# Attention scores: the lower part of the keys on 128 partitions instead of 64

## The chip, the cores and the metric

The kernel runs on one core of a Trainium2 chip. The metric is the device time of one execution in microseconds; the number compared is the median of several runs. A core has the matrix engine (PE, with its weight loads shown apart as PEld), the vector engine (DVE), the scalar engine (ACT), GpSimd (POOL) and the queues that issue DMAs (SP, and those of ACT and POOL).

## The reference

The reference is one inference step of a decoder trunk of two layers. Layer 0 mixes tokens by a gated delta rule, layer 1 by attention in a sliding window; each is followed by a gated MLP, and a norm stands at the end. 512 prompt tokens and 8 samples of 4 tokens go through the same weights, all in float32. What matters here is the prompt's attention: 16 query heads of 64, 4 key heads, blocks of 128 queries that see their own and the previous 128 keys.

```python
s = jnp.einsum('bnqkgd,bnskd->bnkgqs', qb, kk)            # queries x (previous block, own block)
mask = band[None] & ((blkid > 0) | (j[None] >= W))        # band: 0 <= rel <= 128
s = s * SWA_SCALE - alibi_slopes() * rel
m = jnp.maximum(jnp.max(s, -1, keepdims=True), sinks)
p = jnp.exp(s - m); p = p / (p.sum(-1) + exp(sinks - m))
o = jnp.einsum('bnkgqs,bnskd->bnqkgd', p, vv)
```

## The kernel before

Tokens lie along the free axis (544 of them: 512 and 32), features on the 128 partitions. A dense product (`dense`, L140, its matmul at L159) splits each float32 operand into an upper part in the format float32r and the rest, the lower part, and sums three matmuls: upper by upper, upper by lower, lower by upper. Weights come in pieces of 512 columns by DMA (`load_w`, L126) and are split by ACT (L133) and DVE (L135). Tokens are worked in two halves of 256 and 288 columns.

The attention (`attention`, L1125) goes through a plan written out by hand (L39): `kv` projects keys and values, `q0` to `q7` project two query heads each, `a0` to `a7` do the scores, softmax and value product of those two heads, `s0` and `s1` do the samples, `w0` and `w1` the output projection. The framework then orders the instructions of every engine at build time, by its own estimate of when each can start, so that the matmuls of projections come between those of scores. On the chip each engine keeps that order.

In `proj_kv` (L1184) the keys of two heads lie on one tile, 64 partitions each, for a = 0 and 1. `upper` (L1176) makes the upper part on ACT, in one buffer. L1190 subtracts it on DVE and so makes the lower part `kl`, 128 partitions by 2 x 512 columns. L1193 copies the upper part by DMA (four for each a, on the queues of SP and ACT) so that each head c of `kh` holds the same 64 rows twice, on both halves of the partitions. `proj_q` (L1206) lays the queries out to match: for head c the upper part of the queries lies on half c and their lower part on the other half (L1214 to L1216).

In `prompt` (L1221) each block of 128 queries and 128 or 256 keys is then the sum of two matmuls into one place:

```python
PE.matmul(sl, lhsT=q[:, c, ...], rhs=kh[:, c, a, ks], start=True, stop=False)      # L1241
PE.matmul(sl, lhsT=q[rows, c, ...], rhs=kl[rows, a, ks], start=False, stop=True)   # L1242
```

L1241 has 128 rows and gives both products with the keys' upper part; L1242 has the 64 rows of head c, on which the queries' upper part and the keys' lower part lie. There are 64 such pairs, 8 in each of the 8 prompt steps. A score bank (`sc`, two of them) holds two blocks. DVE adds the bias and takes the maximum (L1243); ACT does the exp (L1254); DVE scales (L1264); PE transposes (L1266) into banks that ACT copies out (L1267); PE multiplies with the values (L1272). POOL clears the sample queries' tile (L1152), computes the norm's reciprocal root as a power (L214) and copies sample queries (L1219).

Of the kernel before, what the change touches and what calls it, by code (L numbers as in the profile page):

```python
# [9 lines left out]
F32 = mybir.dt.float32  # L10
F32R = mybir.dt.float32r
BF16 = mybir.dt.bfloat16
AF = mybir.ActivationFunctionType
ALU = mybir.AluOpType

P = 128
SEQ = 512
# [58 lines left out]
def kernel(  # L76
# [315 lines left out]

    ffn(0, 1)
    attention(tc, locals())
    ffn(1, 3)

# [728 lines left out]
def attention(tc, env):  # L1125
    nc, PE, DVE, ACT, POOL = (env[k] for k in ("nc", "PE", "DVE", "ACT", "POOL"))
# [6 lines left out]
    with ExitStack() as ctx:  # L1133
        env["psum_pools"](ctx, acc=ACC, sc=2, pt=PT, po=1, sp=1)
        c1 = ctx.enter_context(tc.tile_pool(name="a1", bufs=1))
# [7 lines left out]
        kT = c1.tile([P, 2, TOK], F32, name="kT")  # L1143

        kh = c1.tile([P, 2, 2, SEQ], F32R, name="kh")
        kl = c1.tile([P, 2, SEQ], F32R, name="kl")
        bqs = c1.tile([P, 8], F32, name="bqs")
        DVE.tensor_scalar(bqs, pc("bqkv", 0, 8), 0.125, None, ALU.mult)
        vt = c1.tile([P, 5, 256], F32, name="vt")
# [5 lines left out]
        def operand(qi):  # L1155

            if qi not in ops:
                if qi < 4:
                    ops[qi] = [c1.tile([P, TOK], F32R, name=f"ao{r}{qi}") for r in "hl"]
                else:  # L1160
                    ops[qi] = [hpool.tile([P, TOK], F32R, tag=f"h{r}{qi}", name=f"ao{r}{qi}") for r in "hl"]
            return ops[qi]

        def proj(m, out, scale=None, tag="acc"):
            ps = dense(w_qkv[m], f"wqkv{m}", hrhs, [8], tag=tag)
            t = tmp("pre", f"qkv{m}")[:, :TOK]
            for p, o, r in halves(ps, t, rstd):
                DVE.tensor_tensor(o, p, r, ALU.mult)
            if scale is None:
                DVE.tensor_scalar(out, t, pc("bqkv", m), None, ALU.add)  # L1170
            else:
                ACT.activation(out, t, AF.Identity, bias=bqs[:, m:m + 1], scale=scale)
# [3 lines left out]
        def upper(t, name):  # L1176
            hi = p2.tile([P, SEQ], F32R, tag="hi", name=f"hi{name}", bufs=1)
            ACT.copy(hi, t)
            return hi

        def spread(out, t, d):
            (nc.sync if d else nc.scalar).dma_start(out.bitcast(F32), t.bitcast(F32))

        def proj_kv():  # L1184
            for a in range(2):
                proj(8 + a, kT[:, a], tag=("acc", "sc")[a])
            nc.gpsimd.dma_start(kT_out, kT[:, :, SEQ - P:TOK])
            for a in range(2):
                hi = upper(kT[:, a, :SEQ], f"k{a}")
                DVE.tensor_tensor(kl[:, a], kT[:, a, :SEQ], hi, ALU.subtract)  # L1190
                for c in range(2):
                    for d in range(2):
                        spread(kh[64 * d:64 * d + 64, c, a], hi[64 * c:64 * c + 64], d)  # L1193
            for a in range(2):
                vT = tmp("y", f"vT{a}")[:, :TOK]
                proj(10 + a, vT)
                nc.gpsimd.dma_start(vT_out[:, a], vT[:, SEQ - P:TOK])
                pv = bank("pt", f"pvt{a}")
                for n in range(NCH):
                    PE.transpose(pv[:, n * P:(n + 1) * P], vT[:, n * P:(n + 1) * P], ident)  # L1200
                ACT.copy(vt[:, 0:4, a * P:(a + 1) * P], pv.rearrange("p (n c) -> p n c", n=NCH))
                pv2 = bank("pt", f"pvs{a}")
                PE.transpose(pv2[:32, 0:P], vT[:, SEQ:TOK], ident)
                ACT.copy(vt[:32, 4, a * P:(a + 1) * P], pv2[:32, 0:P])
# [16 lines left out]
        def prompt(qi):  # L1221

            a, g = qi // 4, qi % 4
            q = q_[qi]
            bias = p2.tile([P, 2, 256], F32, tag="bias", name=f"bias{qi}")
            for c in range(2):
                DVE.tensor_scalar(bias[:, c], ka[:, 0:256], SLOPES[(2 * a + c) * 4 + g], None, ALU.mult)
            s = p2.tile([P, 2, NCH, 256], F32, tag="s", name=f"s{qi}")
            mx = p2.tile([P, 2, NCH], F32, tag="mx", name=f"mx{qi}")
            es = p2.tile([P, 2, NCH], F32, tag="es", name=f"es{qi}")  # L1230
            sm = p2.tile([P, 2, NCH], F32, tag="sm", name=f"sm{qi}")
            for n0 in range(0, NCH, 2):
                for c in range(2):
                    rows = slice(64 * c, 64 * c + 64)
                    h = (2 * a + c) * 4 + g
                    pss = bank("sc", f"ps{qi}_{n0}_{c}")
                    for n in (n0, n0 + 1):
                        k0 = P if n == 0 else 0
                        sl = pss[:, (n - n0) * 256 + k0:(n - n0 + 1) * 256]
                        ks = slice((n - 1) * P + k0, (n + 1) * P)  # L1240
                        PE.matmul(sl, lhsT=q[:, c, n * P:(n + 1) * P], rhs=kh[:, c, a, ks], start=True, stop=False)  # L1241
                        PE.matmul(sl, lhsT=q[rows, c, n * P:(n + 1) * P], rhs=kl[rows, a, ks], start=False, stop=True)  # L1242
                        DVE.tensor_tensor_reduce(  # L1243
                            s[:, c, n, k0:], sl, bias[:, c, k0:], 1.0, pc("sink", h),
                            ALU.add, ALU.max, mx[:, c, n:n + 1])
            for c in range(2):
                h = (2 * a + c) * 4 + g
                DVE.tensor_scalar(es[:, c], mx[:, c], -1.0, pc("sink", h), ALU.mult, ALU.add)
            DVE.tensor_scalar(mx, mx, -1.0, None, ALU.mult)
            ACT.activation(es, es, AF.Exp)  # L1250
            for n in range(NCH):
                for c in range(2):
                    k0 = P if n == 0 else 0
                    ACT.activation(s[:, c, n, k0:], s[:, c, n, k0:], AF.Exp, bias=mx[:, c, n:n + 1],  # L1254
                                   accum_out=sm[:, c, n:n + 1])
            DVE.tensor_tensor(sm, sm, es, ALU.add)
            DVE.reciprocal(sm, sm)
            po = bank("po", f"po1{qi}")
            for n in range(NCH):
                ptp = bank("pt", f"ptp{qi}_{n}")  # L1260
                pT = p2.tile([P, 2, 256], F32, tag="pT", name=f"pT{qi}_{n}")
                k0 = P if n == 0 else 0
                for c in range(2):
                    DVE.tensor_scalar(s[:, c, n, k0:], s[:, c, n, k0:], sm[:, c, n:n + 1], None, ALU.mult)  # L1264
                    for kb in range(k0 // P, 2):
                        PE.transpose(ptp[:, c * 256 + kb * P:c * 256 + (kb + 1) * P], s[:, c, n, kb * P:(kb + 1) * P], ident)  # L1266
                ACT.copy(pT[:, :, k0:], ptp.rearrange("p (c k) -> p c k", c=2)[:, :, k0:])  # L1267
                for c in range(2):
                    rows = slice(64 * c, 64 * c + 64)
                    kv = 2 * a + c  # L1270
                    for kb in range(k0 // P, 2):
                        PE.matmul(po[rows, n * P:(n + 1) * P], lhsT=vt[:, n - 1 + kb, kv * 64:kv * 64 + 64],  # L1272
                                  rhs=pT[:, c, kb * P:(kb + 1) * P], start=(kb == k0 // P), stop=(kb == 1))
            oh, ol = operand(qi)
            ACT.copy(oh[:, :SEQ], po)
            DVE.tensor_tensor(ol[:, :SEQ], po, oh[:, :SEQ], ALU.subtract)
# [65 lines left out]
        def w_out(part):  # L1342
# [13 lines left out]
            if part == 1:  # L1356
                for m in range(4, KD):
                    norm_split(3, m, x[m])

        steps = {"q": proj_q, "a": prompt, "s": sample, "w": w_out}  # L1360
        for step in PLAN_A.split():
            if step == "kv":
                proj_kv()
            else:
                steps[step[0]](int(step[1:]))
# [171 lines left out]
```

## Time and profile before

| | |
|---|---|
| median of 3 runs | 1753.47 us (1748.12 to 1753.71) |
| the profiled execution's own time | 1754.97 us |
| its span | 1753.2 us |
| PE busy | 1648.0 us, 94% of the span |
| PEld busy | 1577.9 us, 90% |
| DVE busy | 947.7 us, 54% |
| ACT busy | 754.0 us, 43% |
| POOL busy | 230.0 us, 13% |
| mean granted clock of PE | 0.961 |

The span runs from the first to the last instruction. Busy times are sums over instructions and overlap between engines. Matmuls overlap each other, and their ends are modelled; the distance between the starts of two matmuls tells the pace of PE better than their durations. The form of a matmul is written as rows*columns of its weights and then rows x columns of what moves through: `64*128 64x256` has 64 rows, 128 columns of weights and 256 moving columns. [...]

### The profile page before, as it was taken

The page shows a single profiled execution, that of the slowest core. Times are in us where ns is not written, and L with a number is a line of the kernel's source. Part 1 is how long each engine was busy: PE and PEld are TensorE (multiplying, and loading weights), DVE is VectorE, ACT ScalarE, POOL GpSimd, SP SyncE. Part 2 cuts the span into 40 slices and gives each one's busy share as a digit, 9 for nine tenths or more (in the row PEclk, how much of TensorE's full clock was granted, in tenths as well). Part 3 has the DMA queues.
Part 4 walks back from the last instruction along what each step waited for, and adds up shares of the span by engine and source line. Part 5 has one row for each costly group of instructions (what it writes and reads, how often), then busy time and mean ns, then how long its engine had stood idle before and what let it go on. Part 6 is the DMA issues. An engine that isn't in the chain of part 4 may idle for free.

```text
span 1753.2 us, 33971 instructions
## 1 busy us (share of the span) xinstructions
PE 1648.0 (94%) x13370; PEld 1577.9 (90%) x13370; DVE 947.7 (54%) x2071; ACT 754.0 (43%) x1822; POOL 230.0 (13%) x474
## 2 busy tenths in 40 slices
PE   7997996898897899999999999999999999999997
PEld 6996896897786798999999999998779999999997
DVE  7985485467465646654444433456566554454333
ACT  5864484474555445433333323245444332332221
POOL 2216118106402500100000000000000000000001
PEclk9998898999898899999999999999799999999999
DMA  6232431442443464622322333443112233223332
GB/s 233 85 82 65 126 100 51 112 138 62 102 155 109 112 195 140 214 89 86 91 90 85 91 87 92 125 138 86 43 43 73 85 91 89 87 87 90 90 88 85
DMA packets 138487, 179.31 MB, mean 102 GB/s; under 512 B 58600, under 2 KB 66840, under 8 KB 136280
## 3 DMA queue, kind: packets, MB, share of 16 engines
q1 hardware_dynamic: 131096, 155.95, 30.7%
q0 software_dynamic: 3104, 14.67, 2.3%
q10 hardware_dynamic: 4128, 6.53, 1.2%
q8 instruction: 105, 1.72, 0.4%
q14 instruction: 54, 0.44, 0.1%
HBM read 146.84 MB, written 25.02 MB: 98 GB/s over the span
## 4 chain that ended last, share of the span: by engine, by line
PE 77%; POOL 7%; DMA 7%; ACT 4%; DVE 3%; issue 2%; SPq 1%; POOLq 0%; ACTq 0%; DVEq 0%
PE wg_p L159 15%; PE wu_p L159 15%; PE wd_p L159 14%; PE win_p L159 5%; PE wo_p L159 5%; PE wqkv_p L159 4%; DMA Lb<-D 3%; PE wz_p L159 3%; POOL Tn L733 3%; PE wao_p L159 3%; POOL subt L731 3%; PE ps L1242 1%; PE po L1272 1%; PE ptp L1266 1%; PE wdl_p L372 1%
## 5 line engine op out<-in xcount | busy, mean ns | idle before, releaser
L159 PE MATMUL wu_p<-hl,wh_wu 128*128 128x256 f32 (+1 forms) x704 | 199.7, 288 | 0.0
L159 PE MATMUL wg_p<-hl,wh_wg 128*128 128x256 f32 (+1 forms) x704 | 199.7, 288 | 0.0
L159 PE MATMUL wg_p<-hh,wl_wg 128*128 128x256 f32 (+1 forms) x704 | 199.2, 287 | 0.0
L159 PE MATMUL wu_p<-hh,wl_wu 128*128 128x256 f32 (+1 forms) x704 | 199.1, 287 | 0.0
L159 PE MATMUL wg_p<-hh,wh_wg 128*128 128x256 f32 (+1 forms) x704 | 198.5, 288 | 0.3 <-DVE g L329 0.3
L159 PE MATMUL wu_p<-hh,wh_wu 128*128 128x256 f32 (+1 forms) x704 | 198.8, 288 | 0.0
L159 PE MATMUL wd_p<-al,wh_wd 128*128 128x256 f32 (+1 forms) x660 | 190.4, 289 | 0.0
L159 PE MATMUL wd_p<-ah,wl_wd 128*128 128x256 f32 (+1 forms) x660 | 190.1, 288 | 0.0
L159 PE MATMUL wd_p<-ah,wh_wd 128*128 128x256 f32 (+1 forms) x660 | 188.1, 285 | 0.0
L135 DVE TENSOR_TENSOR wl_wd<-wr_wd,wh_wd 128x512 fp32r<-128x512 f32 x90 | 58.3, 648 | 151.7 <-ACT wh_wd L133 150.6
L159 PE MATMUL win_p<-hh0n,wh_win 128*128 128x256 f32 (+1 forms) x448 | 134.3, 302 | 2.0 <-ACT pre L541 2.0
L159 PE MATMUL win_p<-hl0n,wh_win 128*128 128x256 f32 (+1 forms) x448 | 135.0, 303 | 0.7 <-DVE hl0n L278 0.7
L159 PEld LDWEIGHTS wg_p<-hh,wh_wg 128*128 128x128 f32 x704 | 132.3, 188 | 0.4 <-DVE g L329 0.4
L159 PEld LDWEIGHTS wg_p<-hh,wl_wg 128*128 128x128 f32 x704 | 132.6, 189 | 0.0
L159 PEld LDWEIGHTS wu_p<-hh,wl_wu 128*128 128x128 f32 x704 | 132.6, 189 | 0.0
L159 PE MATMUL win_p<-hh0n,wl_win 128*128 128x256 f32 (+1 forms) x448 | 132.4, 299 | 0.0
L159 PEld LDWEIGHTS wu_p<-hh,wh_wu 128*128 128x128 f32 x704 | 132.4, 188 | 0.0
L159 PEld LDWEIGHTS wg_p<-hl,wh_wg 128*128 128x128 f32 x704 | 132.4, 188 | 0.0
L159 PEld LDWEIGHTS wu_p<-hl,wh_wu 128*128 128x128 f32 x704 | 132.4, 188 | 0.0
L133 ACT CAST wh_wg<-wr_wg 128x512 fp32r<-128x512 f32 x88 | 54.7, 621 | 178.6 <-PE wu_p L159 130.8
L133 ACT CAST wh_wd<-wr_wd 128x512 fp32r<-128x512 f32 x90 | 52.8, 586 | 174.7 <-PE wd_p L159 153.8
L159 PEld LDWEIGHTS wd_p<-al,wh_wd 128*128 128x128 f32 x660 | 124.1, 188 | 0.0
(452 smaller groups left out, 4506.3 us busy)
## 6 DMA issues: line engine op xcount, KB each, us to landing
wr_wg<-in_w_gu SPq DMA_DIRECT2D x88, 256.0 KB
wr_wu<-in_w_gu SPq DMA_DIRECT2D x88, 256.0 KB
wr_wd<-in_w_dn SPq DMA_DIRECT2D x75, 256.0 KB
wr_win<-in_w_in SPq DMA_DIRECT2D x64, 256.0 KB
Sg<-in_sdelta SPq DMA_DIRECT2D x8, 1024.0 KB
wr_wz<-in_w_in SPq DMA_DIRECT2D x32, 256.0 KB
out_ss<-Sg POOLq DMA_DIRECT2D x8, 1024.0 KB, 5.4
wr_wo<-in_w_out SPq DMA_DIRECT2D x32, 256.0 KB
```

The lines of the kernel that those rows point to most:

```text
L133: ACT.copy(hi[:, :n], raw[:, o:o + n])
L135: DVE.tensor_tensor(lo[:, :n], raw[:, o:o + n], hi[:, :n], ALU.subtract)
L159: PE.matmul(ps[f][:m, :hw(f)], lhsT=wt[:, sl], rhs=xt[:, hc(f)], start=(k0 + j == 0 and wi == 0), stop=(k0 + j == total - 1 and wi == 2),)
L372: PE.matmul(p, lhsT=wt[i][:, sl], rhs=xt[k][:, c], start=(k == 0 and wi == 0), stop=(k == KF - 1 and wi == 2))
L731: POOL.tensor_tensor(tv, Lb[:, j, j + 1:32].unsqueeze(2).to_broadcast([P, r_, w]), Tn[:, j, 0:w].unsqueeze(1).to_broadcast([P, r_, w]), AL ...
L733: POOL.tensor_tensor(Tn[:, j + 1:32, 0:w], Tn[:, j + 1:32, 0:w], tv, ALU.subtract)
L1242: PE.matmul(sl, lhsT=q[rows, c, n * P:(n + 1) * P], rhs=kl[rows, a, ks], start=False, stop=True)
L1266: PE.transpose(ptp[:, c * 256 + kb * P:c * 256 + (kb + 1) * P], s[:, c, n, kb * P:(kb + 1) * P], ident)
L1272: PE.matmul(po[rows, n * P:(n + 1) * P], lhsT=vt[:, n - 1 + kb, kv * 64:kv * 64 + 64], rhs=pT[:, c, kb * P:(kb + 1) * P], start=(kb == k0 ...
```

## The change

The tile of the keys' lower part gets one copy for each of the two heads c, with the other head's 64 partitions zero. POOL writes the zeros once, ahead of the attention's other work. The subtraction on DVE writes head by head, on 64 partitions each. The second score product then reads all 128 rows of the queries, as the first does; the rows that it adds are multiplied by zero. The number of matmuls and their columns stay as they are.

```diff
-        kl = c1.tile([P, 2, SEQ], F32R, name="kl")
+        kl = c1.tile([P, 2, 2, SEQ], F32R, name="kl")
+        for c in range(2):
+            POOL.memset(kl[64 * c:64 * c + 64, 1 - c].bitcast(F32).rearrange("p a s -> p (a s)"), 0.0)
...
             for a in range(2):
                 hi = upper(kT[:, a, :SEQ], f"k{a}")
-                DVE.tensor_tensor(kl[:, a], kT[:, a, :SEQ], hi, ALU.subtract)
                 for c in range(2):
+                    rows = slice(64 * c, 64 * c + 64)
+                    DVE.tensor_tensor(kl[rows, c, a], kT[rows, a, :SEQ], hi[rows], ALU.subtract)
                     for d in range(2):
                         spread(kh[64 * d:64 * d + 64, c, a], hi[64 * c:64 * c + 64], d)
...
                         PE.matmul(sl, lhsT=q[:, c, n * P:(n + 1) * P], rhs=kh[:, c, a, ks], start=True, stop=False)
-                        PE.matmul(sl, lhsT=q[rows, c, n * P:(n + 1) * P], rhs=kl[rows, a, ks], start=False, stop=True)
+                        PE.matmul(sl, lhsT=q[:, c, n * P:(n + 1) * P], rhs=kl[:, c, a, ks], start=False, stop=True)
```

## Rows read from the trace of the kernel before

**Rows 1.** The page: its head, and the chain that ended last by engine.
```profile
span 1753.2 us, 33971 instructions
...
PE 77%; POOL 7%; DMA 7%; ACT 4%; DVE 3%; issue 2%; SPq 1%; POOLq 0%; ACTq 0%; DVEq 0%
```

**Rows 2.** Stretches: length, PE, PEld, DVE, ACT, POOL busy, clock, DMA share, GB/s.
```profile
1160.00:1237.00 77.00, 77.00 (x569) 65.13 (x567) 45.93 (x171) 39.99 (x109) 4.01 (x14) 1.00 0.39 110
1237.00:1268.00 31.00, 30.98 (x158) 21.82 (x159) 17.90 (x89) 13.74 (x49) 0.00 (x0) 0.67 0.01 1
1268.00:1303.00 35.00, 34.81 (x265) 29.05 (x264) 21.40 (x73) 16.76 (x50) 0.00 (x0) 1.00 0.14 46
```

**Rows 3.** PE's longest wait from 1160 to 1320 us: total, times, longest one.
```profile
PE ptp L1266 <- DVE s L1264: 0.9, 1, 0.9
```

**Rows 4.** Timeline of PE (start, duration): a pair of 256 columns among dense matmuls.
```profile
1164.39 0.28 PE L1241 MATMUL ps<-kh,qp 128*128 128x256 f32 x1
1164.60 0.38 PE L1242 MATMUL ps<-kl,qp 64*128 64x256 f32 x1
1164.91 0.40 PE L159 MATMUL wqkv_p<-hh,wl_wqkv 128*128 128x288 f32 x1
1165.14 0.29 PE L159 MATMUL wqkv_p<-hh,wh_wqkv 128*128 128x288 f32 x1
1165.28 0.29 PE L159 MATMUL wqkv_p<-hl,wh_wqkv 128*128 128x288 f32 x1
```

**Rows 5.** Timeline of the weight loads in the same place.
```profile
1164.60 0.18 PEld L1242 LDWEIGHTS ps<-kl,qp 64*128 64x128 f32 x1 [0.15 <-issue]
1165.02 0.19 PEld L159 LDWEIGHTS wqkv_p<-hh,wh_wqkv 128*128 128x128 f32 x1
```

**Rows 6.** The tile `kl`: its readers on PE (ns min/median/max, first and last start).
```profile
L1242 PE MATMUL ps<-kl,qp x64: 322/381/580, 1160.9 to 1302.7; 64*128 64x256 f32 x48, 64*128 64x128 f32 x16
```

**Rows 7.** Timeline of PE: one pair behind another.
```profile
1283.34 0.39 PE L1241 MATMUL ps<-kh,qp 128*128 128x256 f32 x1
1283.66 0.38 PE L1242 MATMUL ps<-kl,qp 64*128 64x256 f32 x1
```

**Rows 8.** Timeline of PE at the lower clock: a pair, and two dense matmuls.
```profile
1240.61 0.58 PE L1242 MATMUL ps<-kl,qp 64*128 64x256 f32 x1
1241.12 0.58 PE L1241 MATMUL ps<-kh,qp 128*128 128x256 f32 x1
...
1264.15 0.41 PE L159 MATMUL wao_p<-aol,wh_wao 128*128 128x256 f32 x1
1264.37 0.41 PE L159 MATMUL wao_p<-aoh,wl_wao 128*128 128x256 f32 x1
```

**Rows 9.** Timeline of PE: a pair of 128 columns.
```profile
1160.72 0.22 PE L1241 MATMUL ps<-kh,qp 128*128 128x128 f32 x1
1160.87 0.32 PE L1242 MATMUL ps<-kl,qp 64*128 64x128 f32 x1
```

**Rows 10.** Groups by form, 1060 to 1340 us: busy us, mean ns, idle before.
```profile
L1254 ACT ACTIVATE s<-s,mx 128x256 f32<-128x256 f32 x48 | 23.7, 497 | 0.0
...
L1243 DVE CUSTOM_DVE_ANT_0 s<-ps,bias,par 128x256 f32<-128x256 f32 x48 | 23.0, 482 | 25.8 <-PE ps L1242 25.3
```

**Rows 11.** The tile `kl`: its writer; then the chain around it (start, duration, what).
```profile
L1190 DVE TENSOR_TENSOR kl<-kT,hik x2: 684/688/693, 1135.0 to 1141.5; 128x512 fp32r<-128x512 f32 x2
...
1135.12 5.59 DMA kh<-hik
...
1141.58 0.57 issue
1142.15 0.46 DVE qkv L1168
```

**Rows 12.** Timeline of POOL (start, duration, idle before and what ended it).
```profile
1119.24 0.53 POOL L1152 MEMSET qd<- 128x512 f32 x1 [384.77 <-PE wd_p L159]
1126.27 1.20 POOL L214 TENSOR_TENSOR ny<-nv,mhalf 128x5 f32<-128x5 f32 x1 [6.50 <-DVE nv L228]
```

## The prediction

> **What bounds the kernel now.** I read first the page's head and its chain of waits, then a table of the attention by stretches, then PE's waits there, then single matmuls. The profiled execution took 1754.97 us, its span 1753.2 [rows 1], so 1.8 us lie around the span; the median of the three runs is 1753.47, 1.5 us below this execution. PE holds 77% of the chain that ended last [rows 1]. The score products (L1241, L1242) all start between 1160 and 1303 us. [...] From 1160 to 1320 the longest wait of PE is 0.9 us, for DVE's scaled probabilities behind the last scores [rows 3]. So PE's own instruction stream sets the time of this stage. A busy PE need not be a PE at its rate; for that I read the distances between starts.
>
> **The price of a 64-row product.** Among dense matmuls two starts lie 0.14 us apart with 288 columns (1165.14 to 1165.28), about 0.13 over a longer row of them. A score pair of 256 columns between them runs 1164.39, 1164.60, 1164.91, 1165.14: 0.21, then 0.31, then 0.23 us for the first dense matmul behind it [rows 4]. The two products and this dense matmul take 0.75 us; by the pace of the dense stream, 0.12 for 256 columns, they would take 0.12 + 0.12 + 0.13 = 0.37. The weight loads say why: a dense load starts about one matmul before its own product (1165.02 for 1165.14), while the load for the 64-row product starts only with that product, at 1164.60 [rows 4, 5]. So a change between the forms 128*128 and 64*128 costs a load that nothing hides: 0.09 us ahead of the 64-row product, 0.19 behind it, and 0.10 behind the next one.
>
> [...]
>
> **The change part by part.** (1) L1242 gets 128 rows. There are 64 such products, 48 with 256 columns and 16 with 128; the last starts at 1302.7 [rows 6]. I went through all distances and sorted them by neighbour:
> - From L1241 to L1242 at the full clock: 26 behind a dense matmul, 0.21 to 0.12 (2.3 us saved); 10 behind another pair, 0.32 [rows 7] to 0.12 (2.0); 19 behind a transpose, a value product or a sample product, where the entering change stays, 0.30 to 0.22 (1.5).
> - From L1242 to the next: 34 to a dense matmul, 0.31 to 0.12 (6.6); 11 to the next pair (2.2); 11 to another form, where one change stays, 0.31 to 0.21 (1.1).
> - The first dense matmul behind a pair: 32 times 0.10 (3.3).
> - At the lower clock: 14 distances, most of them 0.51, where a dense one takes 0.22 [rows 8] (3.2).
>
> The products of 128 columns are in these sums: from the first to the second it is 0.15 now [rows 9], 0.06 under the 0.21 of 256 columns, so I put the full-row one at 0.12 - 0.06 = 0.06. The bounds are 0.06 and 0.12 (no better than 256 columns); with some 30 such distances the other end takes off 1.8 us. Together 22.3 us before rounding: 11.2 of it in 1160 to 1237, 4.5 to 1250, 1.5 to 1268, 5.2 to 1303.
>
> [...]
>
> (2) Not all of the 4.5 us comes through. From 1237 to 1244 ten pairs follow each other with no dense matmul between. Each score block is read by one DVE instruction of 482 ns (256 columns) [rows 10], against 0.63 us per pair now at the full clock and 0.24 then. So DVE takes over there once the two score banks are full: about 0.15 us saved per pair, not 0.4. I take 2.0 of the 4.5; bounds 1 and 4.5. Elsewhere pairs come singly or in twos. Sum: 11.2 + 2.0 + 1.5 + 5.2 = 19.9.
>
> (3) L1190 becomes two half-height subtractions per key tile. One takes 688 ns at 128x512 [rows 11]; for 64 partitions with the same 512 columns I take the same, so DVE gets 1.4 us more. The first tile's stand beside a DMA of 5.59 us that the chain waits for anyway. The second tile's do not: behind them in DVE's queue stands the eviction of a projection (L1168) for which PE waits; the chain runs through 0.57 us spent behind the subtraction and then through that eviction [rows 11]. So one subtraction, 0.6 us, goes on the path; bounds 0 (if the eviction is ordered first) and 1.4.
>
> (4) Two memsets of 64x1024 on POOL. The near row is 128x512 in 0.53 us; by columns each is 1.06, together 2.1. POOL has nothing to do from 1119.8 until DVE hands it the input of its power at 1126.27, and stood idle for 6.50 us before that [rows 12]. That covers them: nothing. Without that cover up to 2.1 us, since the norm's factor waits for this power. POOL's later work (the two output DMAs and the copies of the sample queries) lies behind. No DMA is added or moved: the spreads of L1193 keep their place on SP's and ACT's queues and wait only for ACT. PE's first read of the zeros comes 38 us later. The larger tile (4 KB more per partition) can move other tiles and so early waits: between -1 and +1, taken as 0.
>
> (5) What is late next: PE comes earlier to the transposes (L1266), which wait for exp on ACT and scaling on DVE. The one such wait now is 0.9 us [rows 3]; the dense work ahead of the transposes stays, but each block loses some 1.5 us of cover (four pairs by 0.38). I take 1 us in all; bounds 0 and 6.
>
> Sum: 19.9 - 0.6 - 1.0 = 18.3. The profiled 1754.97 would become 1736.7, and the median 1753.47 becomes 1735.
>
> **Rivals.**
> A, the clock stays up. A mean of 0.67 over 31 us [rows 2] means some 20 us at half, of which the pairs hold about 9; the other 11 (transposes, value and output products) would halve. For it: full-row products leave fewer gaps. Against it: DVE paces the ten pairs, so the columns per us hardly rise there. Gain 18.3 + 5: 1730. Chance 0.10.
> B, the gain is given back in order and waits. The order of instructions is planned when the kernel is built, and the added DVE and POOL work can shift the dense work that now covers exp. A block has eight exps, six of 0.50 us among them [rows 10]; where they stand bare that is some 4.5 us with the scaling, and two such blocks leave 9 us: 1744. Against it: a longest wait of 0.9 us [rows 3]. Chance 0.13.
> C, the row count isn't the price. If the distance came from two products accumulating into one place, or from reading these operands, nothing is saved and 0.6 lost: 1754. Against it: dense matmuls accumulate into one place too, at 0.13, and the late load stands at the 64-row product, not at the dense one [rows 5]. [...] Chance 0.08.
> D, slower: the clock falls earlier. The place is 1207 to 1237, where dense work thins out between transposes and short sample products; the clock now falls at its end [rows 2]. If PE falls to half there from 1207 on, these 30 us of work take 60: 1735 + 30 = 1765. It decides once 24 us of work that now runs at the full clock run at half (18.3 + 5.3). For it: the 0.67 stands right behind; against it: 1.00 over all of 1160 to 1237. [...] Chance 0.06.
>
> **How the numbers follow.** The forecast has 0.63. Its bounds (1.8 for narrow products, -2.5 to +1 for the ten pairs, 0 to 1.4, -1 to +1, 0 to 6) give about 1731 to 1744, since they will not all fall on one side. The range of 1727 to 1747 takes in A and B and leaves out C and D, 0.14, and a little beyond the bounds. What a measurement tells from no change is 0.3%, 5.3 us. Faster: forecast, A and B, 0.86. Same: C, 0.08. Slower: D, 0.06.
>
> **What would show it.** In the changed profile L1242 reads 128*128; in a dense stretch it starts 0.12 us behind L1241, the next matmul 0.12 behind it, its load starts before it, and the first dense matmul behind goes at 0.13. The last score product stands some 18 us earlier than 1302.7. DVE's four subtractions take about 0.69 each, and the memsets end before 1126. It is wrong if distances stay at 0.21 and 0.31 (C), if PE's waits in the stage rise from about 1 us to over 5 (B), or if the clock by stretch differs (A, D).

## The result, and the profile after

The changed kernel takes 1733.49 us in the median of four runs (1728.7 to 1736.2), the kernel before 1753.59 (1748.12 to 1763.09, four runs): a ratio of 0.986, with a 95% interval of 0.9817 to 0.9903, so 17 to 32 us less. The forecast was 1735.0. The profiled execution of the changed kernel took 1736.2 us, that of before 1754.97.

The page of the changed kernel: its head, the busy times, and the chain that ended last by engine. Lines of the code from the memset on have moved: the score products are now L1244 and L1245, DVE's maximum L1246, the transposes L1269.
```profile
span 1734.1 us, 33972 instructions
...
PE 1624.5 (94%) x13370; PEld 1568.9 (90%) x13370; DVE 946.3 (55%) x2073; ACT 754.4 (44%) x1822; POOL 231.1 (13%) x476
...
PE 78%; POOL 7%; DMA 6%; ACT 4%; DVE 3%; issue 2%; SPq 1%; POOLq 0%; ACTq 0%; DVEq 0%
```
PE still bounds the kernel, with as many matmuls as before, and its busy time is 23.5 us shorter. DVE and POOL have two instructions more each, the subtractions and the memsets; what went away is time on PE.

The stretches of the changed kernel in the attention's scores (length, PE, PEld, DVE, ACT, POOL busy, clock, DMA share, GB/s), to be read beside [rows 2]; the last score product now starts at 1283.0 and not at 1302.7.
```profile
1163.70:1220.00 56.30, 56.30 (x475) 53.05 (x475) 40.05 (x149) 34.22 (x94) 3.03 (x12) 1.00 0.41 120
1220.00:1256.00 36.00, 34.50 (x240) 28.12 (x239) 23.98 (x121) 21.73 (x75) 0.41 (x2) 0.76 0.18 52
1256.00:1283.00 27.00, 27.00 (x238) 25.18 (x237) 17.21 (x59) 11.32 (x31) 0.00 (x0) 1.00 0.13 39
```
PE is busy throughout here as before, and the stretch below the full clock is still there, at 0.76 where it was 0.67. From the first score product to the last it was 141.9 us before (from 1160.72) and is 119.2 now (from 1163.76): 22.7 us less. A part of that is order, since 978 matmuls start between the two before and 946 now; the 32 others now stand behind the last score product. In the same two executions the granted clock, read record by record between those products, puts 20.5 us at the lower level before and 17.1 after. The records of these two traces hold two levels alone, 1.00 and 0.50, 19 of each in either; dense matmuls of 256 columns start 0.118 us apart at the first and 0.213 at the second (medians, kernel before).

The timeline of PE in the changed kernel (start, duration): a pair of 256 columns among dense matmuls, then one of 128 columns; these answer to [rows 4] and [rows 9].
```profile
1166.83 0.28 PE L1244 MATMUL ps<-kh,qp 128*128 128x256 f32 x1
1166.95 0.28 PE L1245 MATMUL ps<-kl,qp 128*128 128x256 f32 x1
1167.07 0.30 PE L159 MATMUL wqkv_p<-hh,wl_wqkv 128*128 128x288 f32 x1
1167.20 0.29 PE L159 MATMUL wqkv_p<-hh,wh_wqkv 128*128 128x288 f32 x1
...
1163.76 0.22 PE L1244 MATMUL ps<-kh,qp 128*128 128x128 f32 x1
1163.82 0.28 PE L1245 MATMUL ps<-kl,qp 128*128 128x128 f32 x1
1163.93 0.33 PE L159 MATMUL wqkv_p<-hh,wl_wqkv 128*128 128x256 f32 x1
1164.10 0.28 PE L159 MATMUL wqkv_p<-hh,wh_wqkv 128*128 128x256 f32 x1
```
In the wide pair the distances 0.21, 0.31, 0.23 have become 0.12, 0.12, 0.13: 0.75 us are now 0.37. The weight loads of the same place, beside [rows 5]:
```profile
1166.83 0.19 PEld L1245 LDWEIGHTS ps<-kl,qp 128*128 128x128 f32 x1
1166.95 0.19 PEld L159 LDWEIGHTS wqkv_p<-hh,wl_wqkv 128*128 128x128 f32 x1
```
The load for L1245 starts with the product ahead of it (1166.83) and not any more with its own (1166.95), and the next dense load starts with L1245. No load of this pair lies bare, that is, starts only with its own product.

The tile `kl` of the changed kernel: its reader on PE and its writers (ns min/median/max, first and last start), beside [rows 6] and [rows 11].
```profile
L1245 PE MATMUL ps<-kl,qp x64: 272/279/416, 1163.8 to 1283.0; 128*128 128x256 f32 x48, 128*128 128x128 f32 x16
...
L1194 DVE TENSOR_TENSOR kl<-kT,hik x4: 677/686/690, 1137.2 to 1144.4; 64x512 fp32r<-64x512 f32 x4
...
L1148 POOL MEMSET kl<- x2: 949/951/953, 1121.5 to 1122.5; 64x1024 f32 x2
```
A subtraction on 64 partitions takes what one on 128 took (686 and 688 ns, with 512 columns in both), so the split by heads doubles DVE's work here.

What that costs shows ahead of the scores. The timeline of the changed kernel, DVE and PE, where the second key tile's subtractions stand:
```profile
1143.75 1.39 DVE L1194 TENSOR_TENSOR kl<-kT,hik 64x512 fp32r<-64x512 f32 x2 [2.42 <-ACT hik L1180]
...
1145.17 0.46 DVE L1170 TENSOR_TENSOR qkv<-wqkv_p,rstd 128x288 f32<-128x288 f32 x1
...
1145.68 0.40 PE L159 MATMUL wqkv_p<-hh,wh_wqkv 128*128 128x288 f32 x1 [1.19 <-DVE qkv L1170]
1145.92 0.29 PE L159 MATMUL wqkv_p<-hl,wh_wqkv 128*128 128x288 f32 x1
```
The projection's eviction starts 1.42 us after the subtractions begin (1143.75 to 1145.17), against 0.61 with one subtraction (1141.54 to 1142.15), 0.81 us more, and PE's wait behind it is 1.19 us where it was 0.37 in the kernel before:
```profile
1142.65 0.40 PE L159 MATMUL wqkv_p<-hh,wh_wqkv 128*128 128x288 f32 x1 [0.37 <-DVE qkv L1168]
```
From the end of the MLP ahead of the attention to the first score product it is 42.37 us now and was 41.55.

### The profile page after: what moved, and what is told of

The parts are those of the page before. It is cut to its first block, busy times and chain, and to the rows that moved or that the text cites. A ratio compares the mean times of both kernels' runs of the same rounds, so it can differ in the third digit from the quotient of the medians.

```text
span 1734.1 us, 33972 instructions
## 1 busy us (share of the span) xinstructions
PE 1624.5 (94%) x13370; PEld 1568.9 (90%) x13370; DVE 946.3 (55%) x2073; ACT 754.4 (44%) x1822; POOL 231.1 (13%) x476
## 4 chain that ended last, share of the span: by engine, by line
PE 78%; POOL 7%; DMA 6%; ACT 4%; DVE 3%; issue 2%; SPq 1%; POOLq 0%; ACTq 0%; DVEq 0%
PE wg_p L159 15%; PE wu_p L159 15%; PE wd_p L159 14%; PE win_p L159 5%; PE wo_p L159 5%; PE wz_p L159 4%; PE wqkv_p L159 4%; DMA Lb<-D 3%; PE wao_p L159 3%; POOL Tn L733 3%; POOL subt L731 3%; PE po L1275 1%; PE ptp L1269 1%; PE wdl_p L372 1%; PE gram L684 1%
```

## The experiments

Theory F is the one on record: a 64-row product among 128-row ones pays for a change of form, the change removes it, and the new layout costs about a microsecond. The main rival is C, that something else in the second product sets the distance. Each kernel below leaves one part of the change out or alters one part alone.

**Layout without the rows.** The changed kernel, with the second product on 64 rows again:
```diff
-    PE.matmul(sl, lhsT=q[:, c, n * P:(n + 1) * P], rhs=kl[:, c, a, ks], start=False, stop=True)
+    PE.matmul(sl, lhsT=q[rows, c, n * P:(n + 1) * P], rhs=kl[rows, c, a, ks], start=False, stop=True)
```


> The changed kernel with its new tile, its zeros on POOL and its four subtractions, but the second product again on the 64 rows of its head. Theory F (the changes between the forms 128*128 and 64*128 are the price): distances of 0.21, 0.31 and 0.23 us stand as before, and the time is that of the kernel before plus 0.6 to 2 us: 1754 to 1756, ratio 1.000 to 1.002. Theory O (the gain came from another order of the instructions that the layout brought about): a good part of the 20 us is there without the 128 rows, time under 1745.

Measured: 1757.70 us (10 runs, 1748.39 to 1765.14) beside 1751.41 for the kernel before (19 runs), a ratio of 1.0027 (1.0000 to 1.0053). The timeline of PE:
```profile
1165.29 0.28 PE L1244 MATMUL ps<-kh,qp 128*128 128x256 f32 x1
1165.49 0.38 PE L1245 MATMUL ps<-kl,qp 64*128 64x256 f32 x1
1165.81 0.40 PE L159 MATMUL wqkv_p<-hh,wl_wqkv 128*128 128x288 f32 x1
1166.04 0.29 PE L159 MATMUL wqkv_p<-hh,wh_wqkv 128*128 128x288 f32 x1
```
With the memsets, the larger tile and the two subtractions in place, the distances are those of before: 0.20, 0.32, 0.23. The layout gives nothing by itself. PE's wait for the projection's eviction is there as in the changed kernel:
```profile
PE wqkv_p L159 <- DVE qkv L1170: 1.4, 1, 1.4
```

**Rows without the layout.** The kernel before, with the second product on all 128 rows of the old tile:
```diff
-    PE.matmul(sl, lhsT=q[rows, c, n * P:(n + 1) * P], rhs=kl[rows, a, ks], start=False, stop=True)
+    PE.matmul(sl, lhsT=q[:, c, n * P:(n + 1) * P], rhs=kl[:, a, ks], start=False, stop=True)
```
The 64 rows that it adds hold the queries' lower part times the other head's keys, which the reference does not have.

> The kernel before with 128 rows in the second product and nothing else: it reads the lower part of both heads' keys without zeros, so that it adds the queries' lower part times the other head's keys' lower part, which the reference does not have. No zeros on POOL, two subtractions. Theory F: distances 0.12, 0.12 and 0.13 as in the changed kernel, time as there or 0.6 to 1.5 us less: 1731.5 to 1733.5, ratio to before 0.987. Theory O: the time stays above 1745. If the zeros matter (a lower load on PE, and so its clock), the granted clock is lower here than in the changed kernel.

Measured: 1728.08 us (4 runs, 1726.11 to 1730.32), a ratio of 0.9854 (0.9806 to 0.9902). The stretches of the attention's scores:
```profile
1160.80:1220.00 59.20, 59.20 (x510) 55.30 (x508) 41.06 (x152) 36.29 (x99) 3.40 (x14) 1.00 0.38 114
1220.00:1256.00 36.00, 34.35 (x293) 28.68 (x292) 27.74 (x135) 22.58 (x78) 0.00 (x0) 1.00 0.19 59
1256.00:1273.00 17.00, 17.00 (x150) 16.33 (x148) 12.46 (x44) 7.90 (x25) 0.00 (x0) 1.00 0.15 47
```
One line of code, with DVE's and POOL's work as before, gives the whole gain. In this execution the clock never left the full level in these stretches, and first to last score product took 112.1 us; over the whole execution its mean was 0.968, not below the changed kernel's 0.962, though there are no zeros here. So the rows are the cause, not the tile, the memsets or the subtractions. The framework orders the matmuls anew in each of these kernels, so a share of order is in every comparison of times; a single pair's distances among dense matmuls (0.12, 0.12) are free of it.

**Both products on 64 rows.** If what costs is the change of form and not the 64 rows, two 64-row products behind each other should pay for it once per pair and not within it. The kernel before, with the first product cut to the 64 rows of its head, so that queries' lower part by keys' upper part is left out:
```diff
-    PE.matmul(sl, lhsT=q[:, c, n * P:(n + 1) * P], rhs=kh[:, c, a, ks], start=True, stop=False)
+    PE.matmul(sl, lhsT=q[rows, c, n * P:(n + 1) * P], rhs=kh[rows, c, a, ks], start=True, stop=False)
```


> The kernel before with the first product too on the 64 rows of its head: it leaves out the queries' lower part times the keys' upper part. Both products of a pair then have the form 64*128. Theory F: the two changes of form move to the ends of the pair. Ahead of the pair the last dense matmul takes 0.22 instead of 0.13, the first product 0.22 (0.21 before), the second 0.21 (0.31 before), the first dense one behind 0.23; a pair among dense matmuls costs as much as before, but a pair behind a pair changes nothing, so those go at 0.12 to 0.24 per product and the time falls by 2 to 6 us: 1747 to 1751, ratio 0.996 to 0.999. Theory C (a product of 64 rows is slow by itself, or by what it reads or adds to): both products take 0.31 wherever they stand, and the time grows by 6 us or more: 1759, ratio 1.003.

Measured: 1747.39 us (10 runs, 1735.8 to 1756.18), a ratio of 0.9972 (0.9940 to 1.0005). The timeline of PE:
```profile
1160.17 0.38 PE L1241 MATMUL ps<-kh,qp 64*128 64x256 f32 x1
1160.39 0.28 PE L1242 MATMUL ps<-kl,qp 64*128 64x256 f32 x1
1160.60 0.40 PE L159 MATMUL wqkv_p<-hl,wh_wqkv 128*128 128x288 f32 x1
1160.84 0.29 PE L159 MATMUL wqkv_p<-hh,wl_wqkv 128*128 128x288 f32 x1
```
and its weight loads:
```profile
1160.17 0.18 PEld L1241 LDWEIGHTS ps<-kh,qp 64*128 64x128 f32 x1
1160.28 0.19 PEld L1242 LDWEIGHTS ps<-kl,qp 64*128 64x128 f32 x1
1160.60 0.19 PEld L159 LDWEIGHTS wqkv_p<-hl,wh_wqkv 128*128 128x128 f32 x1
```
The load of the second 64-row product, now behind another 64-row product, starts ahead of its own product (1160.28 for 1160.39); the loads that start only with their own product are the first of the pair (1160.17) and the dense one behind it (1160.60). The median of L1242 falls from 381 ns [rows 6] to 276, though its operands and rows are those of before. So a 64-row load is hidden behind a 64-row product: the price belongs to the change between forms.

For a lone pair among dense matmuls nothing is gained by this, since the pair still goes there and back once: from the start of the dense matmul ahead to the start of the second one behind, the median is 0.87 us before (21 places), 0.89 here (14) and 0.48 in the changed kernel (25). Two other things shorten this kernel. A pair that stands before a value product gives way to it after 0.43 us, where it took 0.62 before. And at twelve places the pairs of the two heads run side by side:
```profile
1267.51 0.39 PE L1241 MATMUL ps<-kh,qp 64*128 64x256 f32 x2
1267.73 0.28 PE L1242 MATMUL ps<-kl,qp 64*128 64x256 f32 x2
1267.94 0.40 PE L159 MATMUL wao_p<-aol,wh_wao 128*128 128x288 f32 x1
```
Each of the first two lines holds two products that start 7 ns apart, and the two pairs together take 0.43 us (1267.51 to 1267.94), as long as one pair above (1160.17 to 1160.60). The products of head 0 lie on the lower 64 partitions and those of head 1 on the upper 64. At eleven of the places the first products of the two heads start within 7 ns of each other, at the twelfth within 61. Twelve pairs that cost nothing are worth some 5 us (12 x 0.43, an estimate), more than half of what this kernel saves. The kernel before has no such place: a 128-row product stands between any two of 64 rows. So the time of this kernel does not price the change of form; the distances and the loads do.

**The subtractions off the path.** In the changed kernel the second tile's subtractions stand late because `upper` has one buffer, which the first tile's copies hold. Here the two tiles have buffers of their own:
```diff
-    hi = upper(kT[:, a, :SEQ], f"k{a}")
+    hi = p2.tile([P, TOK], F32, tag="q", name=f"hik{a}")[:, :SEQ].bitcast(F32R)
+    ACT.copy(hi, kT[:, a, :SEQ])
```


> The changed kernel, with the upper part of the keys in two buffers of the tile that later holds the queries, so that the second one is made without waiting for the DMA of the first (5.59 us). My theory: in the changed kernel PE stands for 1.2 us at the projection of the values because the second subtraction pair, 1.4 us of DVE, starts only after that DMA and stands ahead of an eviction. Without the wait the two subtractions come earlier, PE's wait goes, ACT's wait of 2.5 us too, and the time falls by 1 to 2 us: ratio to the changed kernel 0.999, to before 0.985. Rival: the next thing that is late (the weights' split on ACT) holds PE as long, and the time is that of the changed kernel within 0.3 us; the trace then shows PE waiting for ACT there.

Measured: 1728.68 us (4 runs, 1723.14 to 1734.3), a ratio of 0.9853 (0.9807 to 0.9899). DVE's timeline:
```profile
1131.39 1.38 DVE L1195 TENSOR_TENSOR kl<-kT,hik 64x512 fp32r<-64x512 f32 x2
...
1133.15 1.38 DVE L1195 TENSOR_TENSOR kl<-kT,hik 64x512 fp32r<-64x512 f32 x2
```
Both tiles' subtractions now stand 1.76 us apart, no wait of PE is left from 1115 to 1156, and from the end of the MLP to the first score product it is 40.8 us, 1.5 less than the changed kernel. The wait that the layout brings is thus where step (3) put it, and can be taken away.

**The two once more, side by side.** The changed kernel and the last one again, on one chip:

> The changed kernel once more, unchanged, to see how much of its time hangs on the granted clock of the one execution. In the profile of the changed kernel the clock was at half for about 17 us of 1220 to 1260, in that of the rows alone not at all, with the same forms and nearly the same order. Theory F with a clock that differs between executions: the attention from its first to its last score takes 112 to 119 us, and the less of it is at half clock the shorter, about 0.4 us per us at half; ratio to before 0.985 to 0.990. Rival: the zeros or the new tile cost time there; then the stretch takes 119 us again, whatever the clock.

> The changed kernel with two buffers for the keys' upper part once more, beside the changed kernel on one chip. Its trace showed the first score product 1.5 us earlier, counted from the attention's begin, and no wait of PE at the projection of the values. Expected: 1 to 2 us less than the changed kernel in the median (ratio 0.9990 to it), which the spread of single executions may hide; from the begin of the attention to the first score 40.8 us against 42.4. Rival: the order that it brings about gives more or less than that; then the stretch from the first to the last score differs at equal clock by over 2 us.

Measured: the changed kernel 1728.19 us (5 runs, 1725.71 to 1738.46), ratio 0.9857 (0.9821 to 0.9893); the one with two buffers 1727.63 (6 runs, 1726.23 to 1728.07), ratio 0.9843 (0.9813 to 0.9874); the kernel before 1756.09 (11 runs). The two medians lie 0.6 us apart, and the runs of the changed kernel spread over 12.8, so the better version is not told apart by its time, only by the wait that is gone from its profile. What differs between its two profiles is the clock: in the second the stretch that fell below the full clock reads
```profile
1220.00:1260.00 40.00, 37.70 (x270) 31.11 (x265) 26.13 (x121) 22.28 (x76) 0.00 (x0) 0.83 0.12 33
```
at a mean of 0.83, where the first profile has 0.76 from 1220 to 1256. From its first score product to its last this execution took 118.6 us with 13.7 us at the lower level; the kernel with two buffers took 113.5 with 3.4 in its first profile and 118.6 with 13.7 in its second. The changed kernel's second execution alone doesn't decide against its rival, since 118.6 is close to the 119 us that the zeros or the new tile would give whatever the clock; the 113.5 does, because both are there too.

**Time at equal clock.** To take the clock out, each execution's mean granted clock and span give its microseconds at the lower level, 2 x (1 - clock) x span, with the two levels 1.00 and 0.50 that the records above hold. Over the 73 executions whose clock is known, a line with one slope for all kernels and a level for each fits with a spread of 1.9 us; its slope is 0.40 us of time per microsecond at the lower level. The differences in the last column have standard errors of 0.8 to 1.1 us.

| kernel | runs | mean us at the lower level | level of the line, us | against before |
|---|---|---|---|---|
| before | 30 | 134 | 1700.3 | |
| changed | 9 | 123 | 1682.3 | -18.0 |
| layout without rows | 10 | 143 | 1700.8 | +0.5 |
| rows without layout | 4 | 118 | 1681.2 | -19.1 |
| both on 64 rows | 10 | 143 | 1690.8 | -9.5 |
| changed, two buffers | 10 | 118 | 1680.9 | -19.4 |

At equal clock the change is worth 18.0 us. What the layout costs, 0.5 (layout alone) to 1.1 (rows alone against the changed kernel, 1682.3 - 1681.2), is not clear of these errors. The four first runs of the changed kernel lie 16 us below the level of before and the five later ones 19, so executions differ by more than the clock.

The profiles allow a check that leaves out what the change doesn't touch. Ahead of the attention PE, ACT and DVE run the same instructions in the same order in all eight profiles, and yet that part takes from 1114.6 to 1121.4 us: 1119.2 before and 1121.4 in the first profile of the changed kernel, with 105.8 us at the lower level in both. From there to the end of the span, less 0.40 us for each microsecond at the lower level, it is

| kernel | us from the end of the MLP to the end, at equal clock | against before |
|---|---|---|
| before | 621.1 | |
| changed, two profiles | 602.7, 603.3 | -18.4, -17.8 |
| layout without rows | 622.2 | +1.1 |
| rows without layout | 600.9 | -20.2 |
| both on 64 rows | 613.5 | -7.6 |
| changed, two buffers, two profiles | 600.3, 601.8 | -20.8, -19.3 |

So the 18 us stand in the attention and behind it, and by these single profiles the layout takes 1 to 2 us of what the rows alone give. The kernels whose score products all have 128 rows spent less time at the lower level on average, 118 to 123 us against 134 to 143.

## Why the prediction was right, by its steps

**What bounds, and the price of a 64-row product.** Shown. The layout alone leaves the distances and the time, the rows alone take both away, and with both products on 64 rows the price moves to the edges of the pair. C falls by this: the second product accumulates into the same place in every one of these kernels, and it is slow from the new tile as from the old one as long as it stands alone on 64 rows. Loads start a product ahead on the same 128 rows (1166.83 for 1166.95) and on the same 64 rows (1160.28 for 1160.39); where the form changes they start only with their own product (1164.60 [rows 4, 5]; 1160.17 and 1160.60). Products of 64 rows on the two halves of the partitions ran side by side in the kernel with both products on 64 rows (1267.51 above); in the kernel before they never stand next to each other. Ahead of the load that the change keeps back some time passes, 0.09 us by the distance of 0.21 beside 0.12; what PE does in it, and what keeps the load back, the traces don't show.

Going there and back costs 0.38 us at the full clock, for a 64-row product of 256 columns among dense ones (0.75 - 0.37). The prediction shared this out as 0.09 ahead of the product, 0.19 behind it and 0.10 behind the next one. The rows allow a simpler reading, an estimate: each of the two changes costs about 0.19 (0.38 / 2), of which 0.09 lies ahead of the load and 0.10 comes with the bare load, whose own record has 0.18 to 0.19. A product whose load starts with it has a record longer by 0.10 (0.38 to 0.40 beside 0.28 to 0.29), and the product behind it starts later by as much. That is so without any change of form, where only a wait keeps the load back: the dense product at 1145.68 has 0.40, and the next starts 0.24 behind it and not 0.13.

**Step (1) and (2), the distances.** They were put at 22.3, less 2.5 for the ten pairs that DVE paces: 19.9 after rounding. I added up, in both traces, the distance from each first product to its second, from each second to the next, and of each first dense matmul behind a pair: 46.1 us before (163 distances) and 26.8 after (166), so 19.3 saved. With the layout alone the sum is 46.6, with the rows alone 26.1. In the parts:

- First to second product: 17.3 us before, 10.0 after. Behind dense matmuls 0.12, as forecast; behind transposes 0.20 and behind value products 0.22, where the entering change was said to stay at 0.22. Behind another pair step (1) has 0.12, and it came to 0.22 wherever the first product had waited for its bank: its load waited with it and lies bare (at 1231.99 below the product's record has 0.39). Step (1) left that out.
- Products of 128 columns were the mis-sized term. From the first to the second it is 0.06 behind dense matmuls (1163.76, 1163.82), the value chosen. But the next product stands 0.11 behind the second (1163.93), not 0.06, and the dense product of 256 columns takes 0.17 (to 1164.10) and not 0.12: pair and dense product take 0.34 us, where 0.24 was forecast. With some eight such pairs ahead of dense matmuls this is about 0.8 us, an estimate, about the size of the 0.6 by which the distances fell short.
- The pairs in a row: before, ten of them from 1236.97 to 1244.77, 7.8 us; after, from 1229.99 to 1235.3, 5.3 us. The gain is 2.5 of the 4.5 us, where 2.0 was taken, but not by DVE's pace alone: before, the clock fell to the lower level at 1239.6, with half of these pairs still to come, and after only at 1234.7, ahead of the last one. At the full clock a pair of 256 columns behind another took 0.62 us before, and in this row it takes 0.57 on average, so the 0.15 per pair of step (2) came to some 0.05. DVE does pace them, as PE's waits in the stage show (first line), and as the timeline of such a pair does:
```profile
PE ps L1244 <- DVE mx L1246: 1.3, 5, 0.3
PE wao_p L159 <- ACT aoh L1278: 0.7, 1, 0.7
PE ptp L1269 <- DVE s L1267: 0.4, 1, 0.4
PE po L1275 <- DVE aol L1279: 0.4, 1, 0.4
```
```profile
1231.99 0.39 PE L1244 MATMUL ps<-kh,qp 128*128 128x256 f32 x1 [0.17 <-DVE mx L1246]
1232.21 0.28 PE L1245 MATMUL ps<-kl,qp 128*128 128x256 f32 x1
1232.57 0.38 PE L1244 MATMUL ps<-kh,qp 128*128 128x256 f32 x1
```
Pair to pair it is 0.58 us there (1231.99 to 1232.57), and not the 0.24 that PE alone would need. Step (2) took 0.482 us for DVE's block [rows 10]. Behind each block DVE also reads out the maximum, 0.08 us, and often does a small step of the softmax, so that its blocks start 0.50 to 0.58 apart there (1232.03, 1232.53, 1233.11); step (2) left that out.

**Step (3), the subtraction on the path.** The place was right, the size a little low: 0.6 forecast, 0.81 by the eviction's delay, 0.82 to the first score product, within the bounds of 0 and 1.4. The kernel with two buffers takes the wait away. The distance to the first score product alone would not show it: the kernel with both products on 64 rows, which subtracts as before, has 40.8 us there and not 41.55.

**Step (4), the memsets.** They take 0.95 us each, where 1.06 was put, and stay hidden. The timeline of POOL in the changed kernel:
```profile
1121.45 1.96 POOL L1148 MEMSET kl<- 64x1024 f32 x2 [384.76 <-PE wd_p L159]
1123.47 0.53 POOL L1154 MEMSET qd<- 128x512 f32 x1
```
POOL is done at 1124.0, and the norm's second products (L238) start as long after the MLP's end as before (11.8 us in both).

**Step (5), what is late next.** 1 us was put there, and it didn't come. Of the waits in the answer above, 0.4 and 0.4 stand where the single 0.9 us of [rows 3] was, and the 0.7 for ACT was there in the kernel before:
```profile
PE wao_p L159 <- ACT aoh L1275: 0.7, 1, 0.7
```
Without the waits for the score banks, which belong to step (2), PE waited 2.3 us in the stage before (1160 to 1320) and 1.9 after (1163 to 1303). B's nine microseconds do not show either; all waits of PE together are 3.2 us.

**The clock.** The 30 us of D did not come, but a fall in the place that D named did, for 3.4 us: from 1221.0 to 1224.4 the changed kernel runs at the lower level, behind transposes and sample products of 16 columns and ahead of the ten pairs, where the kernel before fell only among them (1239.6).
```profile
1221.00:1224.40 3.40, 3.40 (x24) 2.54 (x22) 0.92 (x8) 1.62 (x4) 0.41 (x2) 0.50 0.33 88
```
In the whole stage it has 17.1 us at the lower level instead of 20.5 (A's "some 20 us at half"), by the slope 1.4 us less, and 13.7 in its second profile, 2.7 less. So A came in part, and 0.10 was a small chance for it; the mean of the nine executions, 1731.2, lies nearer to A's 1730 than to the forecast. How much of that is the stage isn't shown. Over whole executions the changed kernel has 11 us fewer at the lower level, by the slope 4.4 us, but ahead of the attention, where the instructions are the same, the eight profiles already differ by 14 us (92 to 106). Nor is it shown that 128-row products keep the clock up: two kernels with the same pairs, before and layout without rows, differ by nearly as much (134 and 143), and no run changed the clock alone. That gaps, columns per us or thinner work set the clock, as the arguments for and against A and D have it, was assumed by the author and is not shown.

So the mechanism was right and the total partly luck. The sum of 18.3 stands beside 18.0 at equal clock because its misses cancel: the distances came to 0.6 less than forecast, the subtraction cost 0.2 more, and the 1.0 of step (5) didn't come (19.3 - 0.8, with nothing lost behind it, is 18.5). What the measured medians gain beyond 18 us goes with the clock and with differences between executions.

## What to carry to other kernels

A product with half the rows took no less time by its record here (a median of 276 ns behind another of 64 rows, 279 on 128), and among full-height products it cost more (0.38 us for 256 columns): each change of form delayed a weight load and laid it bare, which shows in the profile as a load that starts with its own product (1164.60) instead of one ahead (1166.83 for 1166.95). Among full-height products it paid to fill the other rows with zeros (18.0 us at equal clock). Half-height products of the two halves right behind each other ran at the same time (0.43 us for two pairs); a kernel whose whole sum is built that way was not run, so which of the two is better isn't shown. Then look at what the padding's own preparation stands in front of in its engine's queue.

## What the runs showed of the hardware that was not expected

The granted clock of this stage differs from one execution to the next of the same kernel: between first and last score product the changed kernel had 17.1 and 13.7 us at the lower level in its two profiles, the one with two buffers 3.4 and 13.7, the one with the rows alone none. At 0.40 us of time each, such microseconds spread the runs of one kernel: those of before, in one series, from 1745.72 to 1763.34, far more than the layout's whole cost. The kernel's order and its instructions alone don't decide it, then; what else does, the runs do not show.

Two 64-row products on different halves of the partitions start 7 ns apart and take the time of one, though they stand behind each other in one engine's stream (1267.51 above). And a load that was kept back, by a change of form (1164.91) or by a wait (1145.68), went with 0.10 us more on the product that it belongs to, 0.40 beside 0.29, which shows in the distance to the product behind: the second dense matmul behind a pair is late by 0.10 [rows 4] though its own load starts ahead of it [rows 5].
